# A two-layer encoder trunk with 585 more products of zeros ahead of the Q projection of layer 1

## The chip, the cores and the metric

One core of one Trainium2 chip runs the program. The metric is the device time of one execution in microseconds (us). The kernel before took 959.64 us, the median of two runs (959.09 and 960.2).

## The reference, cut to what matters

Two layers work on x of 256 rows and 1024 columns, all in float32. Weights are drawn at random; nothing in the result depends on the change described below.

```python
def hybrid_layer(x, ...):
    h = rms_norm(x, g_mix)
    proj = h @ w_in                       # 1024 -> 8704 columns: B, C, X, U, Q, K, V, three gates
    ...                                   # three mixers: short convolution, pooling, windowed attention
    merged = jax.nn.sigmoid(ga) * y_a + jax.nn.sigmoid(gp) * y_p + jax.nn.sigmoid(gt) * y_t
    x = x + merged @ w_o
    h2 = rms_norm(x, g_ffn)
    gate, up = jnp.split(h2 @ w_gu, [D_FF], axis=-1)
    return x + (jax.nn.silu(gate) * up) @ w_down
```

After both layers one more `rms_norm` gives the output.

## The kernel before

**Layout.** Activations lie transposed: 128 features on the partitions, the 256 positions along the free axis. Each weight matrix is cut into blocks of 128 x 128, and `plan_layer` writes down the order in which all blocks of a layer are used. The blocks arrive in that order, 16 to a transfer (`dma_chunk`, 1 MB, three buffers `raw`), on SP's queue.

**A float32 product from three.** `convert` splits eight blocks at a time into a rounded part `hi` (a copy on ScalarE, line 139) and the rest `lo` (a subtraction on VectorE, line 140), with five buffers each. Activations are split in the same way. `mm3` then issues three matmuls for a block, which add up in one PSUM region: `hi` weights with `hi` activations (line 166), `hi` with `lo` (167), `lo` with `hi` (168). Each has 128 x 128 weights, 256 columns of activations, and a weight load of its own, also where two in a row use the same weights. The trace calls the weights `hi` and `lo`, and the activations by their use (`xg` ahead of the norm, `h` behind it).

**Layer and stages.** `mixer` begins with `quad_outer` for K and V (96 matmuls), then `norm_stats` (two small products over `ones`, line 288, and a chain of small operations on ScalarE and VectorE), then the eight Q tiles by `ntile`, with `norm_rows` (line 304) among them, then gates, convolution, pooling, attention and the output product. `ffn` follows. `quad_outer`, `ntile` and the rest are calls in program order; the Tile layer then orders the instructions of each engine by their dependences. `tc.issue_after(ins)` keeps a block's instructions behind `ins` on the engine of `ins`.

**Other products in the trace.** The kernel opens with 25 matmuls on a tile of zeros, `warm` (line 184), whose result `wps` nobody reads. The attention has scores `sc` (weights q, lines 356 and 357), transposes `pt` (128 columns, line 385) and `o` (weights `vt`, line 400).

**Where operands lie.** As the built program lays them out, every row of a `hi` or `lo` block starts 96 bytes past a multiple of 128 bytes of its partition; those of `vt`, q and all activations start 32 bytes past one, and `warm` lies on one. Temporaries of 512 columns (tag `t2`, eight buffers) start 32 bytes past one as well.

Of the kernel before, what the change touches and what calls it, by code (L numbers as in the profile page):

```python
# [8 lines left out]
F32 = mybir.dt.float32  # L9
F32R = mybir.dt.float32r  # L10
# [6 lines left out]
P = 128  # L17
D = 1024
T = 256
# [73 lines left out]
def trunk(ctx, tc, wst, xT, sinkb, rb, invc, gfin, ident_d, out):  # L93
    nc = tc.nc
    V, S, G, PE = nc.vector, nc.scalar, nc.gpsimd, nc.tensor
# [5 lines left out]
    tmp = ctx.enter_context(tc.tile_pool(name="tmp", bufs=2))  # L101
# [5 lines left out]
    def nm(s):  # L107
        uid[0] += 1
        return f"{s}{uid[0]}"
# [60 lines left out]
    last_mm = [None]  # L170

    def half(j):
        return slice(j * T, (j + 1) * T)
# [68 lines left out]
    def pair(pool, tag, bufs, name):  # L242
        t = pool.tile([P, 2, T], F32R, name=nm(name), tag=tag, bufs=bufs)
        return t[:, 0, :], t[:, 1, :]
# [27 lines left out]
    def preload(func, src):  # L272

        d = tmp.tile([P, 1], F32, name=nm("pre"), tag="pre", bufs=2)
        S.activation(d, src, func)

    def rsqrt(r, sd, ms):

        V.reciprocal(r, sd)
        V.tensor_tensor(ms, ms, r, op=ALU.mult)  # L280
        V.tensor_tensor(ms, ms, r, op=ALU.mult)
        V.tensor_scalar(ms, ms, -0.5, 1.5, op0=ALU.mult, op1=ALU.add)
        V.tensor_tensor(r, r, ms, op=ALU.mult)

    def norm_stats(st, func):
        ps = psA.tile([P, 2 * T], F32, name=nm("ps"), tag="A")
        for tb in range(2):
            PE.matmul(ps[:, tb:tb + 1], st["sum"][:, tb * P:(tb + 1) * P], ones, start=True, stop=True)
        q = tmp.tile([P, 8], F32, name=nm("nq"), tag="nq", bufs=2)
        S.activation(q[:, 0:2], ps[:, 0:2], AF.Sqrt, bias=epst, scale=1.0 / D)  # L290
        V.tensor_scalar(q[:, 2:4], ps[:, 0:2], 1.0 / D, EPS, op0=ALU.mult, op1=ALU.add)
        preload(func, q[:, 0:1])
        rsqrt(q[:, 4:6], q[:, 0:2], q[:, 2:4])
        rr = tmp.tile([P, 4], F32R, name=nm("rr"), tag="nr", bufs=2)
        V.tensor_copy(rr[:, 0:2], q[:, 4:6])
        V.tensor_tensor(rr[:, 2:4], q[:, 4:6], rr[:, 0:2].bitcast(F32), op=ALU.subtract)
        st["q"], st["ps"] = rr, ps
# [94 lines left out]
    def att_pv(t, st):  # L392
        pts = st["pt"].pop(t)
        ps = newA("o")
        pr = t // 4
        for j in range(2):
            for kt in range(2):
                vv = vt[kt][:, pr, 2 * j:2 * j + 2].rearrange("p a d -> p (a d)")
                for i in range(2):
                    PE.matmul(ps[:, half(j)], vv, pts[kt][i][:, half(j)], start=(kt == i == 0), stop=(kt == i == 1))  # L400
        h, lo = pair(act, "q", 9, "ao")
        f, o = t1("of"), t1("oo")
        for j in range(2):
            r, other = slice(64 * j, 64 * j + 64), slice(64 - 64 * j, 128 - 64 * j)
            S.activation(o[r], ps[other, half(j)], AF.Copy)
            V.tensor_tensor(f[r], o[r], ps[r, half(j)], op=ALU.add)
        split(h, lo, f)
        st["ao"][t] = (h, lo)


    def t1(name):
        return tmp.tile([P, T], F32, name=nm(name), tag="t1", bufs=10)

    def mixer(l, st):
        xg = st["xg"]
        def kv_out():
            norm_rows(st)
            r = st["r"]

            for p in range(2):  # L420
                kf = t1("kf")
                V.tensor_tensor(kf[:, ::-1], kb[:, half(p)], r, op=ALU.mult)
                for j in range(2):
                    rr = slice(64 * j, 64 * j + 64)
                    other = slice(64 - 64 * j, 128 - 64 * j)
                    kh, kl = kk[2 * p + j]
                    split(kh[rr], kl[rr], kf[rr])
                    S.activation(kh[other], kf[rr], AF.Copy)
            vf = []
            for p in range(2):  # L430
                f = t1("vf")
                V.tensor_tensor(f[:, ::-1], vb[:, half(p)], r, op=ALU.mult)
                vf.append(f)
            return r, vf
# [2 lines left out]
        ast = {"s": {}, "pt": {}, "ao": {}, "bias": {t: load_bias(t) for t in range(3)}}  # L437
        if l:
            norm_stats(st, AF.Exp)
        qs = []  # L440
        for qd in range(2):
            banks = [newB(), newB()]
# [8 lines left out]
            for b in range(2):  # L451
                f = tmp.tile([P, 2, T], F32, name=nm("qf"), tag="t2", bufs=8)
                for j in range(2):
                    V.scalar_tensor_tensor(f[:, j], banks[b][:, half(j)], HEAD_SCALE, r, op0=ALU.mult, op1=ALU.mult)
                    qa, qb = pair(act, "q", 9, "q")
# [40 lines left out]
        for n in range(8):  # L496
# [5 lines left out]
            c, y, z = t1("c"), t1("y"), t1("z")  # L502
# [207 lines left out]
    with tc.issue_after(st["add"].ins):  # L710
        build_bias()
    for l in range(L):
        acc = mixer(l, st)
        st = {"xg": []}
        for j in range(4):
# [56 lines left out]
    assert state["pos"] == len(plan)  # L772


HEAD_SCALE = 0.125
WARM = 25
MH = 1
# [70 lines left out]
```

## Time and profile before

| | |
|---|---|
| median of the runs | 959.64 us |
| the profiled execution | 965.28 us, span of its instructions 963.1 us |
| granted TensorE clock, mean over the span | 0.999 |
| TensorE busy | 952.8 us (99%), 7881 matmuls in the records |
| VectorE, ScalarE, GpSimd busy | 711.3, 551.0, 38.8 us |
| HBM traffic | 184 GB/s over the span |

Busy time of TensorE is counted from the start of a matmul to its modelled end, and the matmuls overlap: one is recorded as about 280 ns long while the next starts after less than half of that. How fast the engine goes is therefore read from the distance of starts, called pitch below, and not from the durations. The counts in a view by windows take in every instruction that overlaps the window, so some two or three that began before it are among them.

### The profile page before, as it was taken

What the parts mean: (1) busy time and instruction counts of PE and PEld (TensorE: products, weight loads), DVE (VectorE), ACT (ScalarE), POOL (GpSimd) and SP (SyncE); (2) the same over time, 40 slices, a digit from 0 to 9 for tenths busy, and PEclk for the clock granted to TensorE, in tenths of its full rate; (3) what the DMA queues carried; (4) which work ended last, traced back from release to release, by engine and by line L of the source; (5) the groups of instructions that cost most, each with busy time, mean ns of one, the idle gap of its engine ahead of it and who ended that gap; (6) DMA issues with size and microseconds to landing.
All of it is one profiled execution on the core that took longest, in us unless ns stands there. A gap on an engine that the chain in (4) does not pass through costs nothing.

```text
span 963.1 us, 19117 instructions
## 1 busy us (share of the span) xinstructions
PE 952.8 (99%) x7881; PEld 939.9 (98%) x7881; DVE 711.3 (74%) x1277; ACT 551.0 (57%) x916; POOL 38.8 (4%) x60
## 2 busy tenths in 40 slices
PE   8999999999999999999999999999999999999997
PEld 8999999999999999999999999999999999999996
DVE  7999998577679955545599998975677698555555
ACT  6866777655456644444477666765545575444444
POOL 5000000000001000000020000000000020000000
PEclk9999999999999999999999999999999999999999
DMA  8656545544554555555543745444555455655541
GB/s 300 251 186 210 202 162 173 198 176 176 203 191 174 178 190 200 179 177 194 197 178 132 246 166 185 148 171 175 181 197 192 176 190 182 218 176 187 197 142 44
DMA packets 26967, 178.17 MB, mean 185 GB/s; under 512 B 3136, under 2 KB 3664, under 8 KB 6656
## 3 DMA queue, kind: packets, MB, share of 16 engines
q1 hardware_dynamic: 24768, 169.99, 49.8%
q0 software_dynamic: 2112, 6.97, 2.5%
q8 instruction: 61, 1.00, 0.4%
q14 instruction: 26, 0.21, 0.1%
HBM read 175.86 MB, written 1.08 MB: 184 GB/s over the span
## 4 chain that ended last, share of the span: by engine, by line
PE 98%; DMA 1%; DVE 0%; ACT 0%; SPq 0%; issue 0%
PE b L167 25%; PE b L166 25%; PE b L168 25%; PE dn L166 2%; PE dn L168 2%; PE dn L167 2%; PE dn L628 2%; PE dn L627 2%; PE dn L626 2%; PE wo L167 2%; PE wo L166 2%; PE o L400 2%; PE wo L168 2%; PE pt L385 1%; PE sc L357 1%; PE sc L356 1%
## 5 line engine op out<-in xcount | busy, mean ns | idle before, releaser
L140 DVE TENSOR_TENSOR lo<-raw,hi 128x1024 fp32r<-128x1024 f32 (+1 forms) x322 | 389.5, 1218 | 200.9 <-ACT hi L139 199.9
L139 ACT ACTIVATE hi<-raw 128x1024 fp32r<-128x1024 f32 (+1 forms) x322 | 335.9, 1051 | 308.4 <-PE b L167 189.7
L166 PE MATMUL b<-h,hi 128*128 128x256 f32 x1344 | 377.4, 281 | 0.0
L168 PE MATMUL b<-h,lo 128*128 128x256 f32 x1344 | 376.0, 280 | 0.0
L167 PE MATMUL b<-h,hi 128*128 128x256 f32 x1344 | 376.0, 280 | 0.0
L166 PEld LDWEIGHTS b<-h,hi 128*128 128x128 f32 x1344 | 255.0, 190 | 0.2
L168 PEld LDWEIGHTS b<-h,lo 128*128 128x128 f32 x1344 | 253.9, 189 | 0.0
L167 PEld LDWEIGHTS b<-h,hi 128*128 128x128 f32 x1344 | 252.4, 188 | 0.2
L166 PE MATMUL b<-xg,hi 128*128 128x256 f32 x448 | 125.2, 280 | 0.9 <-DVE xg L253 0.9
L167 PE MATMUL b<-xg,hi 128*128 128x256 f32 x448 | 124.9, 279 | 0.9 <-DVE xg L256 0.9
L168 PE MATMUL b<-xg,lo 128*128 128x256 f32 x448 | 124.7, 278 | 0.2 <-DVE lo L140 0.2
L167 PEld LDWEIGHTS b<-xg,hi 128*128 128x128 f32 x448 | 84.2, 188 | 1.3 <-DVE xg L256 1.3
L166 PEld LDWEIGHTS b<-xg,hi 128*128 128x128 f32 x448 | 84.2, 188 | 1.1 <-ACT hi L139 1.0
L168 PEld LDWEIGHTS b<-xg,lo 128*128 128x128 f32 x448 | 84.6, 189 | 0.4 <-DVE lo L140 0.4
L166 PE MATMUL dn<-fa,hi 128*128 128x256 f32 x176 | 49.5, 281 | 0.0
L167 PE MATMUL dn<-fa,hi 128*128 128x256 f32 x176 | 49.5, 281 | 0.0
L168 PE MATMUL dn<-fa,lo 128*128 128x256 f32 x176 | 49.5, 281 | 0.0
L369 ACT ACTIVATE s<-s,sm 128x256 f32<-128x256 f32 x64 | 31.7, 497 | 17.5 <-DVE sm L364 17.5
L166 PE MATMUL b<-z,hi 128*128 128x256 f32 x128 | 36.3, 284 | 0.0
L168 PE MATMUL b<-z,lo 128*128 128x256 f32 x128 | 36.0, 281 | 0.0
L166 PE MATMUL b<-ao,hi 128*128 128x256 f32 x128 | 36.0, 281 | 0.0
L167 PE MATMUL b<-ao,hi 128*128 128x256 f32 x128 | 36.0, 281 | 0.0
(176 smaller groups left out, 1494.1 us busy)
## 6 DMA issues: line engine op xcount, KB each, us to landing
raw<-wst SPq DMA_DIRECT2D x158, 1024.0 KB, 4.9
bias<-stab POOLq DMA_DIRECT2D x16, 384.0 KB, 4.5
raw<-wst SPq DMA_DIRECT2D x3, 512.0 KB, 8.0
out<-yg SPq DMA_DIRECT2D x4, 256.0 KB, 2.2
x<-xT SPq DMA_DIRECT2D x3, 256.0 KB, 8.0
raw<-wst SPq DMA_DIRECT2D x2, 256.0 KB, 5.1
gf<-gfin POOLq DMA_DIRECT2D x2, 256.0 KB, 3.1
x<-xT SPq DMA_DIRECT2D x1, 232.0 KB, 2.7
```

The source lines that it names most:

```text
L139: S.activation(hi[:, s], raw[:, s], AF.Copy)
L140: V.tensor_tensor(lo[:, s], raw[:, s], hi[:, s].bitcast(F32), op=ALU.subtract)
L166: PE.matmul(dst, wh, xh, start=start, stop=False, skip_group_check=skip)
L167: PE.matmul(dst, wh, xl, start=False, stop=False, skip_group_check=skip)
L168: last_mm[0] = PE.matmul(dst, wl, xh, start=False, stop=stop, skip_group_check=skip)
L356: PE.matmul(ps[:, half(j)], qs[t][j][:, cs], kh, start=True, stop=False)
L357: PE.matmul(ps[:, half(j)], qs[t][j][:, cs], kl, start=False, stop=True)
L369: S.activation(ss[i // 2][:, i % 2], ss[i // 2][:, i % 2], AF.Exp, bias=sm[:, 4 + i:5 + i], accum_out=sm[:, 12 + i:13 + i])
L400: PE.matmul(ps[:, half(j)], vv, pts[kt][i][:, half(j)], start=(kt == i == 0), stop=(kt == i == 1))
L626: PE.matmul(d, ah[:, cs], wh, start=(k == 0), stop=False)
L627: PE.matmul(d, ah[:, cs], wl, start=False, stop=False)
L628: PE.matmul(d, al[:, cs], wh, start=False, stop=(k == FT - 1))
```

## The change

A new function `probes` sets three tiles `za`, `zb`, `zc` of 128 x 512 to zero on VectorE, takes one PSUM bank `pa`, and issues matmuls on them whose result nobody reads. There are nine rounds, one for each number in `PROBES` (eight numbers, 16 comes twice): the number is the column at which the weights begin in `zb` and `zc`, 4 bytes each. In a round there are five groups, one for each number in `FIRST`: one product of that many columns, then twelve of 256 columns in the order of `mm3` (the same weights twice with two halves of `za`, then weights from `zc` with the first half). So there are 9 x 5 x 13 = 585. The weights thus begin 32 + 4 x `w` bytes past a multiple of 128: at 80, 88, 96, 104, 112, 0, 16, 64 and 96 bytes for the nine rounds.

`probes` is called in layer 1 alone, behind `norm_stats`, and kept behind the last matmul of K and V.

```diff
+    def probes():
+        za, zb, zc = [tmp.tile([P, 2 * T], F32R, name=nm("z"), tag="t2", bufs=8) for _ in range(3)]
+        for z in (za, zb, zc):
+            V.memset(z.bitcast(F32), 0.0)
+        a = newA("pa")
+        for w in PROBES:
+            for f in FIRST:
+                PE.matmul(a[:, :f], zb[:, w:w + P], za[:, :f], start=True, stop=True)
+                for j in (0, 1, 2, 0):
+                    for t, m in ((zb, 0), (zb, T), (zc, 0)):
+                        PE.matmul(a[:, T:], t[:, w + j * P:w + (j + 1) * P], za[:, m:m + T], start=True, stop=True)
...
         if l:
             norm_stats(st, AF.Exp)
+        if l:
+            with tc.issue_after(last_mm[0].ins):
+                probes()
...
+PROBES = (12, 14, 16, 18, 20, 24, 28, 8, 16)
+FIRST = (256, 248, 240, 224, 200)
```

TensorE, where K and V of layer 1 end and Q begins; `b` is the bank that is filled, `ps` the bank of `norm_stats`. Before:

```order
L168 MATMUL b454_6213<-xg450_6204,lo163_6215 128x256
L288 MATMUL ps458_6336<-ones_124,s1452_6210 128x1 x2
L166 MATMUL b462_6352<-xg440_6172,hi164_6244 128x256
L167 MATMUL b462_6352<-xg440_6172,hi164_6244 128x256
L168 MATMUL b462_6352<-xg440_6172,lo164_6245 128x256
```

The same place in the changed kernel: the beginning of the 585, the first products of the second and of a last group, the last three, and the first of Q:

```order
L288 MATMUL ps458_6336<-ones_124,s1452_6210 128x1 x2
L420 MATMUL pa465_6358<-z462_6352,z463_6353 128x256
L423 MATMUL pa465_6358<-z462_6352,z463_6353 128x256 x2
L423 MATMUL pa465_6358<-z462_6352,z464_6354 128x256
...
L420 MATMUL pa465_6358<-z462_6352,z463_6353 128x248
...
L420 MATMUL pa465_6358<-z462_6352,z463_6353 128x200
...
L423 MATMUL pa465_6358<-z462_6352,z463_6353 128x256 x2
L423 MATMUL pa465_6358<-z462_6352,z464_6354 128x256
L166 MATMUL b466_6944<-xg440_6172,hi164_6244 128x256
```

All 585 stand in one piece between the two; what follows on TensorE keeps its order but for `norm_rows`, which now stands right behind the first Q tile and not four matmuls later.

VectorE at the same place; `lo163` belongs to K and V, `lo164` to the first Q tile, `nq` is the chain of `norm_stats`. Before:

```order
L256 SCALAR_TENSOR_TENSOR xg450_6204<-x_107,xg450_6204 128x256
L140 TENSOR_TENSOR lo164_6245<-raw82_6141,hi164_6244 128x1024
L140 TENSOR_TENSOR lo165_6273<-raw82_6141,hi165_6272 128x1024
L140 TENSOR_TENSOR lo166_6303<-raw83_6242,hi166_6302 128x1024
L140 TENSOR_TENSOR lo167_6355<-raw83_6242,hi167_6354 128x1024
L140 TENSOR_TENSOR lo168_6411<-raw84_6300,hi168_6410 128x1024
L291 TENSOR_SCALAR nq459_6339<-ps458_6336 128x2
```

In the changed kernel:

```order
L256 SCALAR_TENSOR_TENSOR xg450_6204<-x_107,xg450_6204 128x256
L416 MEMSET z462_6352 128x512
L140 TENSOR_TENSOR lo164_6245<-raw82_6141,hi164_6244 128x1024
L140 TENSOR_TENSOR lo165_6273<-raw82_6141,hi165_6272 128x1024
L140 TENSOR_TENSOR lo166_6303<-raw83_6242,hi166_6302 128x1024
L416 MEMSET z463_6353 128x512
L416 MEMSET z464_6354 128x512
L140 TENSOR_TENSOR lo167_6947<-raw83_6242,hi167_6946 128x1024
L140 TENSOR_TENSOR lo168_7003<-raw84_6300,hi168_7002 128x1024
L291 TENSOR_SCALAR nq459_6339<-ps458_6336 128x2
```

The three fills stand among the conversions for Q, two of them behind `lo166`; nothing ahead of K and V's last operand has moved. ScalarE, GpSimd and SP have no instruction more or less.

## The prediction

> **What bounds the kernel now.** I read the engines' share of the span first, then the chain of work that ended last, then who waited for whom on TensorE.
>
> ```profile
> PE 952.8 (99%) x7881; PEld 939.9 (98%) x7881; DVE 711.3 (74%) x1277; ACT 551.0 (57%) x916; POOL 38.8 (4%) x60
> PEclk9999999999999999999999999999999999999999
> PE 98%; DMA 1%; DVE 0%; ACT 0%; SPq 0%; issue 0%
> engine line waited for: us in total, times, longest us
> PE wps L184 <- DVE epst L179: 1.2, 1, 1.2
> PE b L167 <- DVE xg L256: 0.9, 2, 0.6
> PE b L166 <- DVE xg L253: 0.9, 1, 0.9
> PE b L168 <- DVE lo L140: 0.2, 1, 0.2
> ```
>
> TensorE is 98% of the chain and waits 3.2 us in all, at the start of the program. Its idle time is 963.1 - 952.8 = 10.3 us. So whatever TensorE is given in addition lengthens the run by its own time, unless something falls due earlier for it; and the four waits shown leave nothing of the kind in layer 1. The question is the pitch of 585 products, from start to start.
>
> The pitch is not one number. The view of the busy time by windows gives it for long stretches of matmuls of 256 columns, as length over count; a record lasts 0.28 us, so 0.28 over the pitch, some 2.4, began before the window and come off the count.
>
> ```profile
> core 0: us, PE busy (x), PEclk, DMA share, GB/s
> 32.75:58.15 25.40, 25.40 (x226) 1.00 0.37 130
> 507.35:532.60 25.25, 25.25 (x225) 1.00 0.40 132
> 58.20:180.00 121.80, 121.80 (x1048) 1.00 0.58 199
> 532.80:654.50 121.70, 121.70 (x1048) 1.00 0.54 188
> 180.00:291.00 111.00, 111.00 (x945) 1.00 0.52 181
> 654.50:765.50 111.00, 111.00 (x945) 1.00 0.51 181
> ```
>
> 25.25 / 222.6 = 113.4 ns, and 111.00 / 942.6 = 117.8 ns: the same instruction, the same width, the full clock, and yet two speeds, each of which holds for hundreds of products. The program lays the weights of both at the same place (96 bytes past a multiple of 128), so the place alone does not choose between them; something at the entry of a stretch does. The pairs of rows also show that it is no accident of an execution: a stage has the same speed in layer 0 and in layer 1.
>
> For weights at other places there are three rows in the timeline: `o` with `vt` (32 past a multiple of 128), the last of the opening products on `warm` (at 0, of zeros like the new ones), and the transposes with 128 columns.
>
> ```profile
> 551.23 0.28 PE L400 MATMUL o<-pl,vt 128*128 128x256 f32 x1
> ...
> 551.95 0.28 PE L400 MATMUL o<-pl,vt 128*128 128x256 f32 x1
> ...
> 4.86 1.11 PE L184 MATMUL wps<-warm 128*128 128x256 f32 x8
> ...
> 544.77 1.04 PE L385 MATMUL pt<-ident,s 128*128 128x128 f32 x8
> ```
>
> From 551.23 to 551.95 stand six steps: 120 ns each. `warm`: (1.11 - 0.28) / 7 = 119 ns. The transposes, half as wide, still take (1.04 - 0.27) / 7 = 110 ns: a new set of weights sets a floor that a narrower product doesn't lower.
>
> **The change part by part.** First the 585 products, TensorE alone, nothing of them beside other matmuls. The two rounds at column 16 have the place of the real weights (96 past a multiple): between 113.4 and 117.8, I take the middle, 115.6. The other seven rounds lie off that place; column 24 lies as `warm` does, 119. For the remaining six (80, 88, 104, 112, 16 and 64 bytes past a multiple) no row stands. Their bounds are 113.4, the fast stretch, and 120, `o`; I take 119, since both rows that lie off the real place are there. Mean: (2 x 115.6 + 7 x 119) / 9 = 118.2 ns, and 585 x 118.2 = **69.1 us**; the ends are 585 x 113.4 = 66.3 and 585 x 120 = 70.2. That these add to nothing and are overwritten (each begins its sum anew) I cost at nothing, as `warm` does the same and lies within the bounds.
>
> 36 of the 45 first products of a group are narrower than 256, by 8 to 56 columns. By the transposes' floor they save at most 36 x (119 - 110) = 0.3 us, or nothing where the loads set the pitch, or they push the following group into the other speed, which the bounds above hold already. I take -0.1.
>
> The Trainium skill ("TensorE: Matmul & The Clock Gate", section "Back-to-back issue gap") gives 256 / 2.4 + 2.5 = 109.2 ns for 256 columns in isolation, and its account of the steps says that loading the next weights takes no read bandwidth from the running matmul; an estimate by that page is 585 x 109.2 = 63.9 us wherever the weights lie. The windows above disagree, 113.4 and 117.8, and the 120 of `o` too; that the speed differs between equal shapes is what such a rule has no room for.
>
> Then the fills on VectorE. TensorE comes to the probes at 495.06, where the first Q matmul stood, and needs `za` and `zb` for the first, `zc` for the third.
>
> ```profile
> 494.69 0.50 PE L288 MATMUL ps<-ones,s 128*128 128x1 f32 x4
> 495.06 0.36 PE L166 MATMUL b<-xg,hi 128*128 128x256 f32 x1
> 490.77 4.62 DVE L140 TENSOR_TENSOR lo<-raw,hi 128x1024 fp32r<-128x1024 f32 x4
> 495.92 1.23 DVE L140 TENSOR_TENSOR lo<-raw,hi 128x1024 fp32r<-128x1024 f32 x1 [0.53 <-ACT hi L139]
> L212 DVE MEMSET kk<- 128x256 f32 x4 | 1.1, 272 | 0.0
> L215 DVE MEMSET up<- 128x272 f32 x2 | 0.6, 285 | 0.0
> ```
>
> 16 columns more cost 13 ns, so 512 columns take about 272 + 256 x 0.8 = 480 ns. The four conversions from 490.77 are `lo164` to `lo167`, 1.155 us each. With a fill ahead and two behind the third: 490.77 + 0.48 + 3 x 1.155 = 494.7, the second fill ends at 495.2, the third at 495.7. TensorE wants `zc` by 495.06 + 0.24 = 495.3 and gets it at 495.7: **0.4 us**, with a wait of some 0.1 at the first product among them. The bounds are 0, if the fills start sooner, and 1.6, if a conversion beside GpSimd takes as long as the one of 2.32 us just before:
>
> ```profile
> 486.21 2.32 DVE L140 TENSOR_TENSOR lo<-raw,hi 128x1024 fp32r<-128x1024 f32 x1
> ```
>
> What queues behind these fills, `lo167`, `lo168` and the chain of `norm_stats`, isn't wanted before the probes are done, 69 us later. VectorE, ScalarE and the weights' transfers run ahead in that time until five `hi`, five `lo` and three `raw` are full, and then stand still. On the way back nothing is late: `rr` for `norm_rows` is long there, and the first five half chunks of Q are ready. A head start is worth nothing either, since TensorE waited for none of them. The buffers that the tiles of zeros hold (three of eight of `t2`) and the bank `pa` (one of four) are next asked for by work that needs a Q tile, so behind the probes in any case.
>
> Last, the rest of layer 1 could leave the probes at another of the two speeds. Between 495 and 507 TensorE ran at 117.8 first and 113.4 then; `norm_rows` and the transposes of V come after, and the pairs of windows show the stages behind them at equal speed in both layers, though what preceded differed. I take 0, with -0.5 to +1.0 for the some 300 products up to the first attention step (222.6 x 4.4 ns = 1.0 if the window from 507.35 turns slow).
>
> **Sum:** 69.1 - 0.1 + 0.4 + 0 = 69.4 us. Against its own profiled execution, 965.28 us (span 963.1, 2.2 around it), that is 1034.7; the runs without a profile have a median 5.6 us lower, 959.64, so I predict **1029.0 us**.
>
> **The rivals.** (a) *Off the real place no collision is left*, and the products run at the transposes' floor: 585 x 110 = 64.4, so 1024.3 with the wait. For it: a speed that depends on how two streams meet may vanish where they don't meet. Against: the two rows off the place are slower, not faster.
>
> (b) *One more delay at crooked places.* Five of the eight columns (12, 14, 18, 20, 28) begin off a multiple of 32 bytes, which no real weights do. The step between the speeds seen, 120 - 113.4 = 6.6 ns, once more on five rounds of 65: 325 x 6.6 = 2.1 us over the upper end 70.2, and with the wait and 1.0 behind, 1033.3. The Trainium skill ("SBUF — State Buffer", "Specifications (TRN2)") speaks for it: it has cachelines of 16 bytes, and each cross to a new line pays; columns 14 and 18 begin in mid line, so that a row of 512 bytes touches 33 lines for 32. No run here shows it.
>
> (c) *The crooked loads take twice as long*, 110 ns becomes 220 and sets the pitch: five rounds, 325 x (220 - 118) = 33 us more, 1062; for columns 14 and 18 alone 130 x 102 = 13, 1042. Nothing in the trace speaks for it but that there is no row of such a load.
>
> (d) *The clock closes on zeros.* The opening products run slowly at first:
>
> ```profile
> L184 PE MATMUL wps<-warm x25: 279/415/579, 1.2 to 5.7; 128*128 128x256 f32 x25
> 3.92 2.06 PE L184 MATMUL wps<-warm 128*128 128x256 f32 x13
> ```
>
> From 1.2 to 3.92 the other twelve take 2.72 / 12 = 227 ns each. At that pitch 585 would take 133 us: 1093. Against: the last ones of the same zeros run at 119, so zeros opened the clock.
>
> (e) *Speeds behind the probes change for good.* The window 654.50 to 765.50 at 113.4 would give 942.6 x 4.4 = 4.1 us back: 1024.9. The pair of rows speaks against it.
>
> (f) *Not slower: the products never run.* If a step between the recorded program and the chip dropped products that nobody reads, all 585 would go, since `pa` has no reader at all; it decides at a single read of `pa`. Price: -69.4, and the time is 959.6 again. Against it stand the 25 records of `wps`, which nobody reads either. Hiding them is no way out: 10.3 us of idle TensorE hold at most 94 products at 110 ns.
>
> **How the numbers follow.** The forecast, 1025 to 1032 by the ends 66.3 and 70.2 with the wait and what lies behind, has 0.72. (a) 0.06, (b) 0.10, (c) 0.07, (d) 0.02, (e) 0.02, (f) 0.01. The range takes in (a), (b) and (e): 1024 to 1034, with 0.9. A change within 2% (19.2 us) is about what a measurement of this kernel can't tell from none; only (f) lies there: 0.01. All other cases are slower: 0.99. None is faster.
>
> **What would show it.** In the changed profile a group of 540 and one of 45 matmuls on `pa` in one piece from about 495 to 564, with a pitch of 115.6 in the two rounds of column 16 and near 119 elsewhere; a wait of TensorE for a fill of `z` of some 0.4 us; the windows behind, moved by 69.4 us, with the counts and lengths of before. It is wrong if a round's pitch lies under 113 or over 120 ns, if the two rounds of column 16 differ from all the others by more than 7 ns, or if a stage behind changes its speed.

## The result and the profile after

The changed kernel took **1029.04 us** (two runs, 1028.93 and 1029.14), the kernel before 959.64; the ratio is 1.072, with an interval of 1.068 to 1.077. The forecast was 1029.0. The profiled execution of the change is one of the two, 1029.14 us with a span of 1027.4. First the engines, the chain of work by engine, and the slices of VectorE and of the HBM traffic:

```profile
PE 1015.4 (99%) x8466; PEld 1001.7 (97%) x8466; DVE 712.6 (69%) x1280; ACT 551.0 (54%) x916; POOL 37.1 (4%) x60
...
DVE  7899997577779555558200999897667789555555
...
GB/s 299 245 181 198 181 186 196 173 176 195 181 148 208 206 202 200 181 195 164 83 1 1 164 206 183 186 161 165 165 204 169 202 137 226 190 206 167 203 164 42
...
PE 93%; DVE 3%; DMA 2%; ACT 1%; issue 1%; SPq 0%; DVEq 0%
```

There are 585 matmuls more and three fills more; the other engines have the work that they had. In the 20th to 22nd slice VectorE and the transfers run ahead until their buffers are full and then stand still, as the prediction said. TensorE does not stand still, and it carries the end.

The new groups by line (count, busy time and mean ns of one, idle time ahead of them):

```profile
L423 PE MATMUL pa<-z,z 128*128 128x256 f32 x540 | 69.0, 281 | 0.0
...
L420 PE MATMUL pa<-z,z 128*128 128x256 f32 (+4 forms) x45 | 12.3, 273 | 0.9 <-DVE z L416 0.9
```

The first four of TensorE's waits, the last of them new (us in total, times, longest):

```profile
PE b L167 <- DVE xg L256: 1.5, 3, 0.6
PE wps L184 <- DVE epst L179: 1.2, 1, 1.2
PE b L168 <- DVE lo L140: 1.0, 2, 0.8
PE pa L420 <- DVE z L416: 0.9, 1, 0.9
```

The nine rounds, as windows of TensorE alone from the first product of a round to the first of the next; columns are the window, its length, TensorE's busy time and count, the granted clock, the DMA share and GB/s:

```profile
490.35:498.19 7.84, 7.84 (x66) 1.00 0.65 254
498.19:505.81 7.62, 7.62 (x68) 1.00 0.01 2
505.81:513.25 7.44, 7.44 (x67) 1.00 0.00 0
513.25:520.92 7.67, 7.67 (x67) 1.00 0.01 2
520.92:528.64 7.72, 7.72 (x68) 1.00 0.00 0
528.64:536.33 7.69, 7.69 (x67) 1.00 0.01 2
536.33:544.11 7.78, 7.78 (x68) 1.00 0.00 0
544.11:551.77 7.66, 7.66 (x67) 1.00 0.01 2
551.77:559.37 7.60, 7.60 (x68) 1.00 0.00 0
490.35:559.37 69.02, 69.02 (x586) 1.00 0.08 30
```

Each round has 65 starts, so its pitch is its length over 65: 120.6 ns (with 0.2 us of entry and wait in it), 117.2, **114.5**, 118.0, 118.8, 118.3, 119.7, 117.8, **116.9**; the bold ones are the two rounds at column 16. The whole block is 69.02 us, 118.0 ns a product, at the full clock.

The forecast was made against the traced execution, and the two traced spans differ by 64.3 us only, not by 69.4. From the first `ps` product to the first Q product the changed kernel takes 70.0 us more (70.4 for 0.37); the rest of the difference lies ahead of the probes. Layer 0's feed-forward stage (`ffn`) in a window of 165 us, before and then after; here and below the columns behind the length are the busy times and counts of TensorE, its weight loads, VectorE, ScalarE and GpSimd:

```profile
315.00:480.00 165.00, 165.00 (x1404) 165.00 (x1403) 99.06 (x119) 77.16 (x99) 0.00 (x0) 1.00 0.53 186
```

```profile
315.00:480.00 165.00, 165.00 (x1458) 165.00 (x1457) 105.18 (x132) 82.39 (x110) 0.76 (x1) 1.00 0.54 192
```

165 / (1404 - 2.4) = 117.7 ns, 165 / (1458 - 2.5) = 113.4 ns. The roughly 1550 products of this stage and of K and V behind it thus took 6.9 us less in the changed kernel, though nothing there was touched. Against that stands a wait near 41 us, in layer 0's Q stage, and a few smaller differences there: 1.2 us more. 70.0 - 6.9 + 1.2 = 64.3.

The pitch of this stage is not fixed by the program. 35 executions of the kernel before, timed beside the experiments, lie at 958.0 to 961.4 (26 of them) or at 965.0 to 968.7 (9). The traced one of before (965.28, long pitch) is of the second kind; an experiment below that left this stage alone, traced at 959.85 us, has the short one. That the pitch of this stage is what parts the two kinds is read from these traces and from two experiments below, some 6 us longer than the change with this stage at the long pitch; the other executions of the kernel before have no trace.

The stages behind the probes, as windows of the changed kernel:

```profile
570.50:596.80 26.30, 26.30 (x234) 26.30 (x233) 25.71 (x50) 19.76 (x35) 0.00 (x0) 1.00 0.36 127
597.00:718.50 121.50, 121.50 (x1046) 121.50 (x1045) 106.21 (x254) 80.91 (x177) 3.62 (x5) 1.00 0.53 189
718.70:829.70 111.00, 111.00 (x945) 111.00 (x944) 75.86 (x125) 58.57 (x82) 0.00 (x0) 1.00 0.50 181
```

26.30 / 231.5 = 113.6, then 116.4, then 117.8 ns: the speeds of before in the same order. Nothing was given back there.

### The profile page after: what moved, and what is told of

The parts are those of the page before. It is cut to its first block, busy times and chain, and to the rows that moved or that the text cites. A ratio compares the mean times of both kernels' runs of the same rounds, so it can differ in the third digit from the quotient of the medians.

```text
span 1027.4 us, 20294 instructions
## 1 busy us (share of the span) xinstructions
PE 1015.4 (99%) x8466; PEld 1001.7 (97%) x8466; DVE 712.6 (69%) x1280; ACT 551.0 (54%) x916; POOL 37.1 (4%) x60
## 4 chain that ended last, share of the span: by engine, by line
PE 93%; DVE 3%; DMA 2%; ACT 1%; issue 1%; SPq 0%; DVEq 0%
PE b L167 22%; PE b L166 22%; PE b L168 22%; PE pa L423 6%; PE dn L646 2%; PE dn L645 2%; PE dn L167 2%; PE dn L644 2%; PE dn L168 2%; PE dn L166 2%; DMA raw<-wst 2%; PE wo L166 1%; PE wo L167 1%; PE o L400 1%; PE wo L168 1%; PE pt L385 1%
## 5 line engine op out<-in xcount | busy, mean ns | idle before, releaser
L423 PE MATMUL pa<-z,z 128*128 128x256 f32 x540 | 69.0, 281 | 0.0
L423 PEld LDWEIGHTS pa<-z,z 128*128 128x128 f32 x540 | 66.8, 189 | 0.1
```

Of the source, the lines that this page charges most:

```text
L423: PE.matmul(a[:, T:], t[:, w + j * P:w + (j + 1) * P], za[:, m:m + T], start=True, stop=True)
```

## The experiments

The time was right, but the pitch in it was a middle between bounds, not a known cause. The open question is what sets a pitch of 113.3, 117.8 or 120 ns for the same instruction. In the rounds of the change only column 16 ever settles at 113.3, and only in some groups: after 256, 240, 224 and 200 columns the first time, after 248 alone the second. So my theory was **two stable pitches at the real pair of places, chosen by how a stretch is entered, and one mixed pitch at other places**. The rivals: the widths themselves, the column number, the values multiplied, and the weights' place alone.

Each kernel that only changes the probes was run once, with its trace; their block is read from its trace and not from the whole time.

**Widths at column 16 alone**, all 585 products with 15 first widths, three times:

```diff
-PROBES = (12, 14, 16, 18, 20, 24, 28, 8, 16)
-FIRST = (256, 248, 240, 224, 200)
+PROBES = (16, 16, 16)
+FIRST = (256, 252, 248, 244, 240, 236, 232, 228, 224, 216, 208, 200, 192, 160, 128)
```

> 585 products as in the change, but all at column 16 (the place of the real weights), in 45 groups whose first product has 15 widths from 256 down to 128, the list gone through three times. Theory 1 (place and entry: at this place two speeds hold, 113.3 and 117.8 ns, and the width of the first product shifts the entry): each group settles at one of the two, never near 120; a width gives the same outcome each time it is met in the same speed; 248 and 240 change the speed, 224 and 200 leave it; the block takes 66.3 to 69 us. Theory 2 (chance chooses at each entry): the same two speeds, but a width met again in the same speed gives now one, now the other. Theory 3 (the place alone sets the pitch): all groups alike.

Measured: 1028.99 us, the block 67.9 us. Every one of the 45 groups settles at 113.3 or at 117.8 ns, none between, and all three times are alike group for group: 113.3 after 256, 248, 240, 236, 228, 224, 192 and 128 columns, 117.8 after 252, 244, 232, 216, 208, 200 and 160. Four rows of its timeline, the tail of one time and the head of the next:

```profile
510.85 0.23 PE L420 MATMUL pa<-z,z 128*128 128x160 f32 x1
510.92 1.61 PE L423 MATMUL pa<-z,z 128*128 128x256 f32 x12
...
513.87 0.28 PE L420 MATMUL pa<-z,z 128*128 128x256 f32 x1
513.98 1.52 PE L423 MATMUL pa<-z,z 128*128 128x256 f32 x12
```

Twelve starts are eleven steps and one record of 0.28 us: (1.52 - 0.28) / 11 = 113 ns behind the 256, and 121 behind the 160, where the first step of 156 ns is in the mean and the rest lie at 117.8. The same twelve products on the same bytes differ by what went before them.

**Column 16 with 256 columns throughout**, so that nothing disturbs the stretch (`PROBES = (16,) * 9`, `FIRST = (256,) * 5`):

> 585 products at column 16, and every first product 256 columns wide like the rest, so that nothing in the block shifts the entry. Theory 1 (place and entry): after the first some ten products one speed holds to the end, 113.3 (block 66.3 us) or 117.8 (68.9 us). Theory 2 (chance at each group): the speed changes between groups of 13, about 67.6 us. Theory 3 (place alone): one speed too, and the same one as the mean of the widths' run.

Measured: 1026.56 us, the block 66.5, at 113.3 ns from the second group to the end:

```profile
490.94 1.52 PE L423 MATMUL pa<-z,z 128*128 128x256 f32 x12
492.30 0.28 PE L420 MATMUL pa<-z,z 128*128 128x256 f32 x1
492.42 1.52 PE L423 MATMUL pa<-z,z 128*128 128x256 f32 x12
```

Once in the short pitch, an even stream of one shape stays there; 585 x 113.4 = 66.3 was the prediction's lower bound, and it is reached but for the entry.

**Column 24, place 0, throughout** (`PROBES = (24,) * 9`), with the five widths of the change:

> 585 products with the widths of the change, all at column 24, where the weights begin on a multiple of 128 bytes. Theory 1 (only the place of the real weights has the fast speed): no group settles at 113.3; the mean is that of this round in the changed kernel, 118.4 ns, the block 69.3 us. Rival (the speed comes from what ran just before, not from the place): with five widths in nine rounds some groups run at 113.3, and the block takes 66.3 to 68.5 us.

Measured: 1031.17 us, the block 69.3. Behind the first, the rounds alternate between 117.7 and 118.4 ns, and no group is under 116.9. One of the quicker rows:

```profile
514.34 1.57 PE L423 MATMUL pa<-z,z 128*128 128x256 f32 x12
```

So the five widths alone don't bring the short pitch: with the weights at this place it does not occur.

**Other values**: the three tiles hold rounded copies of x and not zeros.

```diff
-        for z in (za, zb, zc):
-            V.memset(z.bitcast(F32), 0.0)
+        for i, z in enumerate((za, zb, zc)):
+            V.tensor_copy(z, x[:, 2 * i:2 * i + 2].rearrange("p k t -> p (k t)"))
```

> The change as it is, but the three tiles hold rounded copies of x in place of zeros. Theory (the pitch is a matter of addresses and entry, not of values): each round within 1 ns of the changed kernel, column 16 again the only one with groups at 113.3; the block 69 us, plus up to 1 us more waiting, since a copy of 512 columns takes longer than a fill. Rival (zeros run at a pitch of their own): the rounds differ by more than 1 ns all in one direction, or the granted clock falls below 0.99, and the time moves by over 1 us beyond the wait.

Measured: 1028.45 us. But for the first round, which holds a longer wait for the copies, every round is within 0.1 ns of the change's (114.5 and 116.8 at column 16). Zeros and these values run alike, so zeros were a fair stand-in.

**The activations moved by 64 bytes.** Do the two places act together (theory 1a, their distance modulo 128) or the weights' alone (1b)?

```diff
-PROBES = (12, 14, 16, 18, 20, 24, 28, 8, 16)
+PROBES = (0, 0, 0, 16, 16, 16, 24, 8, 24)
...
-                PE.matmul(a[:, :f], zb[:, w:w + P], za[:, :f], start=True, stop=True)
+                PE.matmul(a[:, :f], zb[:, w:w + P], za[:, 16:16 + f], start=True, stop=True)
...
-                    for t, m in ((zb, 0), (zb, T), (zc, 0)):
+                    for t, m in ((zb, 16), (zb, 240), (zc, 16)):
```

> The 585 products, but their 256 moving columns begin 64 bytes further on (96 past a multiple of 128 in place of 32), with three rounds of weights at 32 past a multiple, three at 96 and one each at 0, 64 and 0. Theory 1a (what counts is the distance of weights and moving columns; the real products have 64): the three rounds at 32, whose distance is 64 again, have groups at 113.3, as column 16 has in the changed kernel, and those at 96 (distance 0) have none. Theory 1b (the place of the weights alone counts): the rounds at 96 keep their 113.3, and those at 32 have none. In both the block takes 68 to 70 us.

Measured: 1034.99 us, with layer 0's feed-forward at the long pitch. No group settles under 116 ns: not with weights at 32 (three rounds, 117.5 to 117.6 without the first), not at 96 (117.0 to 117.7), not at 0 or 64. One of the quickest rows, with (1.56 - 0.28) / 11 = 116 ns:

```profile
542.32 1.56 PE L423 MATMUL pa<-z,z 128*128 128x256 f32 x12
```

Weights at 96 are the weights of column 16, so 1b fell, and with it the column number alone; the pair 96 and 32 swapped has the same distance modulo 128, so 1a fell as well.

**The real activations moved by 64 bytes** in the kernel before, by 16 columns less of padding ahead of x, in the tile that holds x; the arithmetic stays what it was:

```diff
-NG = L * 6 * KT + 112
+NG = L * 6 * KT + 96
```

> The kernel before without any extra product, with 16 columns less padding ahead of x, which moves all activations, q and vt from 32 to 96 past a multiple of 128 while the real weights stay at 96: their distance falls from 64 to 0. Theory 1a (the distance counts): the long stretches at 113.4 ns are gone, the real products run at 117 to 120 throughout; in the changed kernel some 3600 products ran at 113.3, so some 3600 x 5 = 18 us more, 975 to 985 us. Theory 1b (the place of the weights alone): the same stretches as before, 959 to 966 us.

Measured: **980.06 us**, against 959.68 for the kernel before beside it (median of 13, 958.05 to 968.74). Windows of layer 0's mixer and feed-forward:

```profile
191.00:288.00 97.00, 97.00 (x820) 97.00 (x819) 67.14 (x113) 48.20 (x67) 0.00 (x0) 1.00 0.52 185
316.00:480.00 164.00, 164.00 (x1385) 164.00 (x1384) 99.22 (x120) 77.39 (x102) 0.00 (x0) 1.00 0.53 185
```

97 / 817.6 = 118.6 and 164 / 1382.6 = 118.6: one pitch for both, and nowhere in the trace a stretch at 113. The weights lie where they lay, with the activations on the same 96 bytes past a multiple of 128, and the short pitch is gone from the whole kernel, at a price of 20 us or 2.1%. This is one run, but the distance is six times the width of the lower group of before (958.0 to 961.4).

**One product to lift a stretch.** The mixer's last part runs 948 products at 117.8 in either layer. If 248 columns lead from the long pitch to the short, as the change showed, one such product there should win about 923 x 4.4 = 4 us a layer. The result of the extra product is overwritten by the next.

```diff
-            ntile(l, "in", CGP + n, hs, b0[:, half(0)])
+            ntile(l, "in", CGP + n, hs, b0[:, half(0)], kick=KICK if n == 0 else 0)
...
+KICK = 248
```

Here and below, `ntile` begins with one more product if `kick` is set, on the weights and activations that come next:

```diff
+        if kick:
+            c, j = divmod(state["pos"], HT)
+            PE.matmul(dst[:, :kick], his[c][:, j * P:(j + 1) * P], xs[koff][0][:, :kick], start=True, stop=True)
```

> The kernel before, with two products more, one a layer: ahead of the first gate tile of the mixer's last part, where the stretch of 948 products at 117.8 ns is under way, a product of 248 columns with that tile's own weights and activations, overwritten by the tile. Theory 1 (entry sets the speed of a stretch, and 248 columns lead from the slow to the fast one, as in the changed kernel's rounds): the some 920 products behind it run at 113.3 in both layers, 2 x 920 x 4.4 = 8.1 us less, 0.25 us more for the two products: about 7.9 us faster than the kernel before at the same speed of the other stages. Rival (a long stretch has the speed of its operands, whatever precedes it): 0.2 us slower.

Measured: 961.0 us (10 runs), ratio 1.002, interval 0.999 to 1.005: no gain. In its trace the stretch stayed long:

```profile
190.00:288.00 98.00, 98.00 (x834) 98.00 (x834) 66.97 (x112) 50.68 (x71) 0.00 (x0) 1.00 0.53 189
```

98 / 831.6 = 117.8. A map by which a width alone takes one pitch to the other fell with it.

**The map, width by width**: column 16, and for nine widths v the groups v, v, 248, v, v.

```diff
+PROBES = (16,)
+FIRST = tuple(f for v in (192, 128, 228, 236, 64, 208, 32, 160, 252) for f in (v, v, 248, v, v))
```

> 585 products at column 16 in 45 groups; nine widths of the first product, each met twice, then one of 248 columns, then twice again, so that most are met from both speeds. Theory 1: every width leads from a given speed to one and the same, in all its occurrences, and 192 and 128 lead from slow to fast as in the widths' run; the block takes 65.5 to 68.5 us (the narrowest first products are shorter). Rival (chance): the same width from the same speed gives both.

Measured: 1030.12 us. Entered from the short pitch, a width had the same outcome each time it occurred in this kernel and in the first one: 192, 208, 224, 236 and 256 columns stay short, 252, 248, 244, 232, 228, 216, 160, 128, 64 and 32 go long (192, 208 and 32 were entered so only once). Entered from the long pitch, the same width gives both: 192 went long once and short four times, 248 short after 236, 64 and 252 but long after 228, 32 and 160. That would fit a long pitch that covers more than one hidden position and a short one that is a single position; no row shows the position itself. 128 and 228 led from long to short every time they met it, five times each, too few to call a rule.

**Only the distance?** The last form of theory 1a: 64 bytes from activations to weights, tried exactly, and at other multiples. Activations 64 bytes on as above, and

```diff
+PROBES = (32, 32, 32, 48, 64, 96, 0, 40, 96)
```

so that the weights lie 64 bytes behind them, as the real ones do, in the first three rounds, then 128, 192, 320, -64, 96 and 320.

> The 585 products with the moving columns 64 bytes further on again, and the weights at columns whose distance from the moving ones is +64 bytes (three rounds, column 32), 128, 192, 320, -64, 96 and 320. Theory 1a, mended (a distance of +64 counts, and -64 is another one): the three rounds of column 32 have groups at 113.3, the round at -64 none, as in the run before; whether 192 or 320 have them tells whether the pattern repeats after 128 or 256 bytes. Theory 1b, mended (the pair of absolute places counts, moving at 32 and weights at 96): no round has a group at 113.3, all lie at 116.5 to 120. The block takes 67.5 to 69.5 us by the first, 68.5 to 70 by the second.

Measured: 1035.67 us, again with layer 0's feed-forward at the long pitch. The rounds lie at 117.4 to 118.1 ns without the first, no group settles under 116.9:

```profile
513.54 1.57 PE L423 MATMUL pa<-z,z 128*128 128x256 f32 x12
```

The distance fell too. Of all that was tried the short pitch occurs only with the activations 32 and the weights 96 bytes past a multiple of 128. The activations were tried at two places only, 32 and 96; why this pair, stays open.

**Nine products instead of one.** From the short pitch 192 stays short; so 192 may be repeated until it takes, at 0.11 us each. I put three into each mixer's last part (128 as the first of layer 1) and three into layer 0's feed-forward stage:

```diff
+            ks = KICKS[l] if n == 0 else (0, 0, 0)
-            ntile(l, "in", CGP + n, hs, b0[:, half(0)])
-            ntile(l, "in", CGT + n, hs, b0[:, half(1)])
+            ntile(l, "in", CGP + n, hs, b0[:, half(0)], kick=ks[0])
+            ntile(l, "in", CGT + n, hs, b0[:, half(1)], kick=ks[1])
...
+            ntile(l, "t", n, [ast["ao"][t] for t in range(8)], b1[:, half(1)], kick=ks[2])
...
+                          kick=192 if l == 0 and q == 1 else 0)
...
+KICKS = ((192, 192, 192), (128, 192, 192))
```

> The kernel before with nine products more, overwritten by what follows: three at the first three tiles of the mixer's last part, 24 products apart, in each layer (192, 192, 192 columns in layer 0, 128, 192, 192 in layer 1), and three of 192 at the second gate and the two up tiles of layer 0's first FFN steps. In the map of widths 192 led from the fast speed to the fast one, and from the slow one to the fast at the latest at the second time; 128 led from slow to fast each time. Theory 1, mended (the slow speed has more than one position, so a single product may leave it slow, but repeated ones end in the fast speed and stay): the mixers' stretches run at 113.3 behind the third product at the latest, 2 x 870 x 4.4 = 7.7 us less and 1.1 us more for the nine: 6.5 us faster than the kernel before where its FFN of layer 0 is fast (959.7), and the slow FFN (966 to 968) no longer comes up. Rival (the speed of so long a stretch comes from its operands and banks): no stretch changes, 1.1 us slower.

Measured: **952.58 us** (5 runs, 951.18 to 953.49) against 960.3 (8 runs, 958.0 to 966.31) for the kernel before beside it; ratio 0.992, interval 0.989 to 0.995. The gain is small, 0.8%, but clear of its interval. Both mixers' last parts and the feed-forward stage:

```profile
191.00:288.00 97.00, 97.00 (x858) 97.00 (x857) 69.94 (x117) 51.08 (x72) 0.00 (x0) 1.00 0.55 195
316.00:480.00 164.00, 164.00 (x1449) 164.00 (x1448) 103.62 (x123) 81.88 (x107) 3.21 (x3) 1.00 0.53 187
656.00:753.00 97.00, 97.00 (x858) 97.00 (x858) 69.94 (x117) 51.15 (x72) 0.00 (x0) 1.00 0.55 195
```

97 / 855.6 = 113.4 where before had 117.8. In layer 0 the second 192 took, in layer 1 the 128, and the later ones left the short pitch as it was. Some 899 and 923 products then run at it: 1822 x 4.4 = 8.0 us less, nine products of some 0.11 us more, so -7.0, and -6.9 is what stands between 952.58 and the median (about 959.5) of the six lower runs of before. In this trace the feed-forward stretch stayed long behind its first extra product and turned short behind its second. None of the five runs is 6 us longer than the others; five are too few to say that this stage now always runs short. This kernel beats both, with more work than the one before.

**`vt` on the weights' place.** The `o` products had 120 ns with weights at 32 past a multiple. Here `vt` lies 64 bytes on:

```diff
-    vt = [act.tile([P, 2, 4, 64], F32R, name=f"vt{kt}") for kt in range(2)]
+    vt = [act.tile([P, 2 * T + P], F32R, name=f"vt{kt}")[:, 16:16 + 2 * T].rearrange("p (k j d) -> p k j d", k=2, j=4) for kt in range(2)]
```

> The kernel before, with vt moved on by 64 bytes (and padded so that everything else keeps its place within 512 bytes), so that the products o have the distance of the real ones, +64, in place of 0. Theory 1 (the distance decides whether the fast speed exists): the o products leave 120 ns and run at 113 to 118. As they are what precedes each slow stretch of the mixer, the stretches behind them are entered differently: if o passes the fast speed on, the long ones of 948 products run at 113.3 and the kernel takes 950 to 953 us; if the scores and transposes before o leave it slow, o runs at 117.8 and the time stays at 959 to 961. Rival (o is slow for what it multiplies, not for where vt lies): o stays at 120 and the time too.

Measured: 958.18 us (10 runs, 957.39 to 959.83), ratio 0.9965, interval 0.994 to 0.999; the kernel before had 13 runs beside it, ten of them around 960.0 and three of the longer kind, and the ratio takes in all. In its timeline the eight `o` products of one step:

```profile
105.42 0.28 PE L400 MATMUL o<-ph,vt 128*128 128x256 f32 x1
105.53 0.28 PE L400 MATMUL o<-pl,vt 128*128 128x256 f32 x1
...
106.32 0.28 PE L166 MATMUL b<-h,hi 128*128 128x256 f32 x1
```

0.90 / 8 = 113 ns instead of 120. At its old place `vt` broke the short pitch: before, the products behind `o` run at 117.8 in all 16 steps of the attention, also where those ahead of it run at 113.3. At the new place `o` hands on what it finds: in ten steps 113.3 ahead, in `o` and in the 48 products behind; in the other six, the last of each layer among them, 117.7 ahead, 117.6 to 117.8 in `o`, and long behind. So the long stretch of the mixer's last part did not turn. The attention of layer 1, TensorE alone, with one record fewer than in its window of before (121.70 us):

```profile
526.40:646.75 120.35, 120.35 (x1047) 1.00 0.54 189
```

128 `o` products of 4.5 ns less in the mean are 0.6 us, ten stretches of 48 x 4.4 ns are 2.1; from the first to the last of the same products it is 121.6 before and 120.3 now, in either layer. The whole time shows less of these 2.7 us, 1.8 against the ten lower runs of before; a stretch ahead of layer 0's second norm ran long in this trace and short in that of before (0.3 us), and the rest was not followed.

**The fills asked for early**, ahead of K and V, for the wait:

```diff
+        zs3 = zeros() if l else None
         kb, vb = quad_outer(l, "in", ...
...
-                probes()
+                probes(*zs3)
```

> The change, with the three fills asked for ahead of K and V of layer 1, so that all three stand ahead of lo164 on VectorE. Theory (the wait of TensorE at the first probe, 0.9 us in the changed kernel, is for the second and third fill, which stood behind three conversions of 1.15 us): the fills end 3.4 us sooner, the wait is gone, and from the first ps product to the first Q product it takes 69.0 us where the changed kernel took 70.0. Rival (the first probe waits for its bank or for the products before it): the gap of 0.9 us stays.

Measured: the wait is gone. The waits of TensorE in this kernel have no row for `pa`, and the first probe follows the `ps` products as Q did before:

```profile
489.21 0.50 PE L288 MATMUL ps<-ones,s 128*128 128x1 f32 x4
489.57 0.37 PE L422 MATMUL pa<-z,z 128*128 128x256 f32 x1
```

From the first `ps` to the first Q product are 69.3 us (489.21 to 558.54), in the change 70.4 (488.97 to 559.37): the fills cost 1.1 us. The whole time of one run, 1029.2, does not show it; other waits, at the program's start, differ by as much between executions.

## Why the prediction was right, step by step

**The bound.** Right. From the first `ps` product to the first of Q before 0.37 us, now 70.4, and the spans behind that point agree: the first Q product comes 64.31 us later in the traced execution, and the span is 64.3 longer. No slack took any of it. That the sum met the median to 0.1 us is luck all the same: the block and its wait cost 70.0 by the traces where the sum had 69.4, and the lower kind of execution alone spreads over 3.4 us.

**The 585 products, 69.1 us.** Measured 69.0, and 68.8 without what belongs to the wait and the entry. The two column 16 rounds have (114.5 + 116.9) / 2 = 115.7 for 115.6, by luck of the entries: the widths experiment shows either pitch for a group, and 256 columns throughout would have given 113.3. The middle of two values was a mean over a mixture, not a value that a group takes. The other rounds have 117.2 to 119.7, a mean of 118.3 behind the first, for 119; `o` and `warm` were fair rows for them, 0.7 ns high. The first round's 120.6 is over the bound of 120 that I set; it holds 0.2 us of wait and entry, and its groups settle at 117 to 118.

**The narrower first products, -0.1 us.** No run measures them alone, but their own time is small: at column 16 a group that one of these widths leads takes 113.3 to 114.0 ns a product where it stays short, and 117.2 to 117.5 for 117.8 where it stays long, so at most 0.3 us for 36 groups. The floor of 110 that I read from the transposes does not hold for a single narrow product: after 200 columns the next start comes 92 ns later, after 32 columns 28 ns, and the step behind is longer (135 and 200). What the widths do is choose the pitch of what follows, and the bounds had that.

**The fills, 0.4 us.** The mechanism is right and the term was too small: 1.1, within its bound of 1.6. VectorE and then TensorE in the timeline of the changed kernel:

```profile
485.84 0.48 DVE L416 MEMSET z<- 128x512 f32 x1
486.24 3.42 DVE L140 TENSOR_TENSOR lo<-raw,hi 128x1024 fp32r<-128x1024 f32 x3
489.72 1.02 DVE L416 MEMSET z<- 128x512 f32 x2
...
488.97 0.50 PE L288 MATMUL ps<-ones,s 128*128 128x1 f32 x4
490.35 0.36 PE L420 MATMUL pa<-z,z 128*128 128x256 f32 x1 [0.88 <-DVE z L416]
```

The fill takes the 0.48 us that I took for it, and the order is the one forecast; but I timed TensorE's arrival and VectorE's by one traced execution, and in this one TensorE stands 0.8 us earlier against VectorE. With the early fills the wait and the 1.1 us are both gone.

**What lies behind, 0.** Right: the three windows have the speeds of before.

**From the traced execution to the median, -5.6 us.** The subtraction was right, but what it stood for was missed. "The pairs of rows also show that it is no accident of an execution" is the sentence that fell. It held for the third pair of windows that I quoted; of the first two, the member in layer 0 differs between traces, by waits of up to 1.3 us and by a stretch near 60 us that has either pitch (0.4 us). And it did not hold for layer 0's feed-forward stage, whose pitch differs between executions: its 6.9 us are about what parts the two kinds. Had the two runs shown been of the other kind, the forecast would have been 7 us off, beyond the range.

**The rivals.** (a) No place freed the products to 110. (b) No price for crooked places: columns 14 and 18, which begin in mid line, have 117.2 and 118.0, the quickest and an average one of the seven off the real place. So the rule of 16-byte lines in the Trainium skill ("SBUF — State Buffer", "Specifications (TRN2)") shows no cost here for weights whose row touches one line more. (c) No load of double length. (d) The clock was 1.00 in every round, and real values gave the same pitches as zeros. (e) Not behind the probes, though such a change of speed does occur elsewhere. (f) All 585 are in the records.

The best pitch that any stretch of such products held is 113.3 ns. The Trainium skill ("TensorE: Matmul & The Clock Gate", "Back-to-back issue gap") gives 109.2 for 256 columns in isolation, an estimate from its formula; no run here reached it.

## What to carry to other kernels

Read a matmul's cost from the distance of starts, stage by stage, and compare a stage's pitch between executions before calling a difference of under 1% an effect of an edit. Where the operands lie can matter more than small edits: here 64 bytes cost 2.1%, so a change of any tile's size ahead of the activations may move the whole kernel. Where, as here, a long stretch holds the longer of two pitches, a few extra overwritten products at its entry may lift it; which width does so has to be tried and read from the trace.

## What the runs showed that was not expected

Identical matmuls (128 x 128 weights, 256 columns, float32 in this rounded form) on identical bytes have two stable pitches, 113.3 and 117.8 ns, for hundreds of products, at the full clock, for zeros and for copies of x alike. One product of another width between them decides which: the outcome was the same each time from the short one, and from the long one it also hangs on something that these traces don't show. The short pitch occurs only for one pair of operand places among those tried; at the others the groups settle at 116 to 121. The probes write one PSUM bank and the real products several, and both kinds show both pitches. What in the chip keeps this state, and why layer 0's feed-forward stage, as the times suggest, enters it differently in 9 of 35 executions, was not settled.
